# Two blocks of modulation rows of the even layer summed on VectorE instead of multiplied on TensorE

## Chip, cores and metric

One core of one Trainium2 chip. The metric is the device time of one execution in microseconds (us): three runs of a kernel and their median, and beside them one execution under the profiler, whose rows are quoted here.

## What is computed

The reference is a trunk of two layers over 512 tokens of width 1024. Each layer first turns the conditioning vector into six rows of modulation; rows 0 and 1 shift and scale the input of the mixer, row 2 gates its output, rows 3, 4 and 5 do the same for the experts.

```
c_act = jax.nn.silu(c)
for layer in range(DEPTH):
    mod = c_act @ ada_w[layer] + ada_b[layer]
    shift1, scale1, gate1, shift2, scale2, gate2 = jnp.split(mod, 6, axis=-1)
    h = modulate(rmsnorm(x, norm1_w[layer]), shift1, scale1)
    # layer 0: pooling mixer and chunked attention, layer 1: Mamba-2 mixer
    x = x + gate1[:, None, :] * mix
    h2 = modulate(rmsnorm(x, norm2_w[layer]), shift2, scale2)
    ffn = hier_moe(h2, ...)
    x = x + gate2[:, None, :] * ffn
```

`ada_w[layer]` is 1024 x 6144 in float32. The kernel cuts it into three parts of 2048 columns: part 0 holds shift1 and scale1, part 1 gate1 and shift2, part 2 scale2 and gate2.

## The kernel before

Everything is one program of five engines that run their own instruction streams in order and wait for each other by semaphores. The order within an engine is set once, when the program is built: a scheduler places the instructions by the order of the code and by its own costs. Only SP, ACT and POOL issue transfers.

**The even mixer** (`even_mixer`) works on four pairs of attention heads. For pair m it projects `q` and `k` (`Dense.next`, tiles `pdq`, `pdk`, 24 matmuls each, L449 to L452), forms the scores (`scores`, tile `sc`, L682), does the softmax (DVE L685 to L690, ACT L688), transposes the probabilities (`transp`, tile `ptr`, L700, copied out by ACT as `ptT`, L702), multiplies by the values (`values`, tile `po`, L711) and splits the result into a high and a low part (`c`, ACT L111 and DVE L112). Four pooling channels (tiles `pdu`, `pl`, `py`) lie between. Projection weights are split in the same way (`q3h`, `q3l` and the like; each third low part of this stage is done on POOL). At the end `out_proj` multiplies slices of the output weight (`mor`) by the gate row (L492), splits them (`mow0h`, `mow0l`) and multiplies on TensorE (tile `mo`).

**The modulation rows** come from the generator `ada(layer, part, eng)`, whose steps the calls of `fill()` drop between the steps of the mixer, by the table `FILL`. One block of 2048 columns is eight slices of 128 rows, 1 MB each, loaded two ahead into a ring of five buffers (tag `w8`). With `eng` None a step is one call of `ada_mm`: four matmuls, one for each 32 output partitions, that accumulate in the PSUM tile `pada`. With an engine given, the step is a running sum in place on that engine, and after one more step the partitions are summed by four matmuls with a matrix of ones:

```
if k:
    a = eng.scalar_tensor_tensor(ws[k], ws[k], ccol[:, k:k + 1], ws[k - 1], op0=ALU.mult, op1=ALU.add)
else:
    a = eng.tensor_scalar(ws[0], ws[0], ccol[:, 0:1], None, op0=ALU.mult)
```

Behind it, in both forms, DVE adds the bias (L215, tile `adab`). Part 0 then goes through four transposes (`pm`, L306) into the columns `ab` of `mod_cols`; parts 1 and 2 are written to the DRAM tile `modd`, and part 2 ends in `router_prep`, which reads `modd` back (`mc`), multiplies (`plb`, L249) and scales the router weights on DVE (L251). The bias tile `adab` and the gate row of `out_proj` share one buffer (tag `rows`). The expert weights `w_0_1` to `w_0_5` of the next stage use the same five `w8` buffers.

Part 1 of layer 0, part 2 of layer 0 and part 0 of layer 1 are computed in the even mixer, one after the other.

Of the kernel before, what the change touches and what calls it, by code (L numbers as in the profile page):

```python
# [76 lines left out]
def trunk_kernel(ctx, tc, x, c, ada_w, ada_b, norm1_w, norm2_w, mix_w_in, pool_w, pool_scale,  # L77
# [4 lines left out]
    V, S, GP, PE, SP = nc.vector, nc.scalar, nc.gpsimd, nc.tensor, nc.sync  # L82
# [7 lines left out]
    def w8(shape, name):  # L90
        return wp.tile(shape, F32, tag="w8", name=name, bufs=W8)
# [10 lines left out]
    def ps(shape=(P, 512), name="ps"):  # L102
        return pp.tile(list(shape), F32, tag="ps", name=name)

    def load_after(ins, first):

        if first is not None:
            tc.add_manual_dep(ins.ins, first.ins.name, SYNC, reason="load_after")
# [56 lines left out]
    def ada_mm(p, k, w, first, last):  # L165

        for q in range(4):
            PE.matmul(p[32 * q:32 * q + 32, :], ccol[:, k:k + 1].to_broadcast([P, 32]), w[:, q * 512:(q + 1) * 512],  # L168
                      start=first, stop=last, skip_group_check=True)

    def ada(layer, part, eng, first=None):


        rows = small.tile([P, D], F32, tag="rows", name=f"adab{layer}{part}", bufs=1)
        b = rows[:, 0:512]
        GP.memset(b, 0.0)
        SP.dma_start(b[0:P:32, :], ada_b[layer, part * 2048:(part + 1) * 2048].rearrange("(b n) -> b n", n=512))
        if part == 2:
            router_loads(layer)
            n2 = rows[:, 512:D]  # L180
            GP.memset(n2, 0.0)
            SP.dma_start(n2[0:64:32, :], norm2_w[layer].rearrange("(b n) -> b n", n=512))
        ws = {}

        def load(k):
            if k < KD:
                ws[k] = w8([P, 2048], f"ada{layer}{part}{k}")
                load_after(SP.dma_start(ws[k], ada_w[layer, k * P:(k + 1) * P, part * 2048:(part + 1) * 2048]), first)

        load(0)  # L190
        load(1)
        p = None
        for k in range(KD):
            load(k + 2)
            yield
            if not eng:
                if not k:
                    p = ps(name=f"pada{layer}{part}")
                ada_mm(p, k, ws.pop(k), k == 0, k == KD - 1)
                continue  # L200
# [4 lines that stand above are left out]
            if k in PIN:  # L205
                tc.keep_in_program_order(a)
        for _ in range(SLACK if eng else 0):
            yield
        if eng:
            p = ps(name=f"pada{layer}{part}")  # L210
            for q in range(4):
                PE.matmul(p[32 * q:32 * q + 32, :], ones[:, 0:32], ws[KD - 1][:, q * 512:(q + 1) * 512], start=True,
                          stop=True, skip_group_check=True)
        m = b
        V.tensor_add(m, p, b)  # L215
        if part == 0:
            mod_cols(layer, m)
        elif part == 1:
            SP.dma_start(modd[layer, 1], m[0:P:32, :])
        else:  # L220
            SP.dma_start(modd[layer, 2, 2:4], m[64:P:32, :])
            V.scalar_tensor_tensor(n2, m, 1.0, n2, op0=ALU.add, op1=ALU.mult)
            SP.dma_start(modd[layer, 2, 0:2], n2[0:64:32, :])
            yield from router_prep(layer)
# [5 lines left out]
    def router_loads(layer):  # L230
        d = rt[layer] = {"wr": small.tile([P, KD, NLOG], F32, tag="wr", name=f"wr{layer}", bufs=1)}
        d["mc"] = small.tile([P, 2, KD], F32, tag="mc", name=f"mc{layer}", bufs=1)
        d["lb"] = small.tile([P, NLOG], F32, tag="lb", name=f"lb{layer}", bufs=1)
        GP.memset(d["wr"], 0.0)
        GP.memset(d["lb"], -BIG)
        SP.dma_start(d["wr"][:, :, 0:4], moe_w_group[layer].rearrange("(p k) g -> p k g", k=KD))
        SP.dma_start(d["wr"][:, :, 8:NLOG], moe_w_expert[layer].rearrange("(p k) g e -> p k (g e)", k=KD))
        SP.dma_start(d["lb"][:, 0:4], dap(moe_b_group, 4 * layer, [[0, P], [1, 4]]))
        SP.dma_start(d["lb"][:, 8:NLOG], dap(moe_b_expert, 32 * layer, [[0, P], [1, 32]]))

    def router_prep(layer):
        d = rt[layer]
        for q, off in enumerate((4096, 3072)):
            SP.dma_start(d["mc"][:, q, :], dap(modd, layer * 6144 + off, [[KD, P], [1, KD]]))
        for _ in range(SLACK2):
            yield
        p = ps((P, NLOG), name=f"plb{layer}")
        for k in range(KD):
            PE.matmul(p, d["mc"][:, 1, k:k + 1].to_broadcast([P, P]), d["wr"][:, k, :], start=k == 0, stop=k == KD - 1)  # L249
        V.tensor_add(d["lb"], p, d["lb"])  # L250
        V.tensor_mul(d["wr"], d["wr"], d["mc"][:, 0, :, None].to_broadcast([P, KD, NLOG]))  # L251
# [51 lines left out]
    def mod_cols(layer, m):  # L303
        p = ps((P, 4, P), name=f"pm{layer}")
        for q in range(4):
            PE.transpose(p[:, q, :], m[:, q * P:(q + 1) * P], ident)  # L306
        A = ab[:, layer, 0, :].rearrange("p (b q) -> p b q", b=2)
        B = ab[:, layer, 1, :].rearrange("p (b q) -> p b q", b=2)
        V.scalar_tensor_tensor(A, p[:, :, 64::32].rearrange("p q b -> p b q"), 1.0,
                               n1w[layer].rearrange("p (b q) -> p b q", b=2), op0=ALU.add, op1=ALU.mult)  # L310
        V.tensor_copy(B, p[:, :, 0:64:32].rearrange("p q b -> p b q"))
# [201 lines left out]
    def even_mixer(layer):  # L513
        with ExitStack() as es:
# [217 lines left out]
            order = (0, 1, 4, 5, 6, 2, 7, 3)  # L732
            c_hi, c_lo = ({k: cs[n // 2][:, n % 2, q, :] for n, k in enumerate(order)} for q in range(2))

            adas = [ada(0, 1, None), ada(0, 2, None), ada(1, 0, None)]

            fills = iter(FILL)

# [716 lines left out]
    def odd_mixer(layer, prev):  # L1455
# [361 lines left out]
        return moe  # L1817

    moe = odd_mixer(1, even_mixer(0))
    fw = []  # L1820

# [55 lines left out]
```

## Time and profile before

| | us |
|---|---|
| three runs | 1078.89, 1082.63, 1082.91 |
| median | 1082.63 |
| the profiled execution, its own time | 1078.06 |
| its span, first to last instruction | 1076.4 |

The span is divided among stages: the even mixer ends and the output projection begins at about 203 us, the experts of layer 0 follow from about 272 us, the odd mixer from about 450 us. A row of a timeline gives the start, the duration, the engine, the line, what is written and read, how many instructions are merged, and in brackets how long the engine had been idle before and what ended that.

### The profile page before, as it was taken

To read this page: it belongs to the slowest core of one execution; us is meant where nothing else is said; L and a number is where in the kernel's file an instruction comes from. 1 tells how busy PE (TensorE), PEld (TensorE's weight loads), DVE (VectorE), ACT (ScalarE), POOL (GpSimd) and SP (SyncE) were. 2 spreads that over 40 slices of the span, in tenths; PEclk is the share of its full clock that TensorE was granted. 3 is DMA by queue.
4 is the path that set the end of the run, shared out by engine and by line. 5 is a ranking of instruction groups with operands and counts; after the bars stand their busy time and mean duration, and the time that the engine had idled before them with its cause. 6 is when DMAs were issued, how large, how long until landed. Compare 5 with 4: busy or idle time off the path is not lost. (4 is left out here: it accounts for less than half of the span.)

```text
span 1076.4 us, 15960 instructions
## 1 busy us (share of the span) xinstructions
PE 975.1 (91%) x5700; PEld 718.9 (67%) x5700; DVE 667.7 (62%) x1476; ACT 440.6 (41%) x893; POOL 219.9 (20%) x284
## 2 busy tenths in 40 slices
PE   5799998897899997899899999999969997998994
PEld 4576655686665656777787777878748876665653
DVE  3523443445556875758976699686766655654874
ACT  3434433324223235247475564664723234222332
POOL 3002110305231134200220131121130005221134
PEclk9899999998899999999999999999989998899997
DMA  8689856697799979547764387454236754799987
GB/s 313 240 280 313 287 219 268 243 369 255 234 386 414 409 210 298 187 122 229 236 182 129 107 235 245 127 150 144 79 118 222 267 194 159 261 411 414 411 258 182
DMA packets 137840, 263.88 MB, mean 245 GB/s; under 512 B 17555, under 2 KB 79975, under 8 KB 132632
## 3 DMA queue, kind: packets, MB, share of 16 engines
q1 hardware_dynamic: 126760, 235.36, 62.6%
q0 software_dynamic: 8928, 20.97, 7.4%
q10 hardware_dynamic: 2064, 6.42, 1.5%
q8 instruction: 49, 0.80, 0.3%
q14 instruction: 39, 0.32, 0.1%
HBM read 254.15 MB, written 20.11 MB: 255 GB/s over the span
## 5 line engine op out<-in xcount | busy, mean ns | idle before, releaser
L1063 PE MATMUL ph<-w,xT 128*64 128x256 f32 (+1 forms) x1152 | 132.0, 373 | 1.9 <-DVE xT L1047 1.6
L1063 PEld LDWEIGHTS ph<-w,xT 128*64 128x64 f32 x1152 | 86.4, 139 | 53.1 <-ACT xT L1049 9.5
L1065 ACT ACTIVATE th<-ph 128x128 f32<-128x128 f32 x34 | 9.4, 277 | 154.1 <-PE pht L1074 136.7
L1084 PE MATMUL pyy<-w,hidT 128*64 128x512 f32 x272 | 65.9, 605 | 2.2 <-ACT hidT L1076 2.2
L1030 POOL DMA_INDIRECT xg<-xnd,toks x32 | 32.2, 1007 | 150.8 <-PE pxt L1042 114.8
L1646 POOL TENSOR_TENSOR ms<-ms,cbm 128x512 f32<-128x512 f32 x16 | 27.1, 1709 | 167.9 <-DVE cbm L1618 116.9
L1049 ACT ACTIVATE xT<-pxt,mc 128x128 f32<-128x128 f32 x136 | 51.1, 456 | 17.4 <-PE pxt L1042 11.9
L1089 DVE SCALAR_TENSOR_TENSOR y<-pyy,wsl,gate 128x512 f32<-128x512 f32 x68 | 48.1, 745 | 9.2 <-DMA yd<-y 7.5
L1042 PE MATMUL pxt<-ident,xg 128*128 128x128 f32 x272 | 37.9, 284 | 15.0 <-DVEq L1415 8.6
L1047 DVE TENSOR_SCALAR xT<-pxt,mc 128x128 f32<-128x128 f32 x136 | 46.7, 405 | 1.4 <-PE pxt L1042 1.4
L1042 PEld LDWEIGHTS pxt<-ident,xg 128*128 128x128 f32 x272 | 34.5, 194 | 15.5 <-issue 15.1
L1115 DVE TENSOR_TENSOR x<-x,pyc 128x512 f32<-128x512 f32 x48 | 30.5, 684 | 22.6 <-DMA x<-yd,row 18.3
L1066 DVE SCALAR_TENSOR_TENSOR th<-th,ph 128x128 f32<-128x128 f32 x34 | 9.8, 287 | 55.2 <-ACT th L1065 55.2
L1631 ACT ACTIVATE ms<-lb,acs 128x128 f32<-128x128 f32 x128 | 40.0, 391 | 5.9 <-DMA lb<-acd 5.9
L1716 POOL TENSOR_TENSOR yy<-yy,yt 128x384 f32<-128x384 f32 x16 | 20.0, 1255 | 102.2 <-DVE yt L1714 81.2
L1595 DVE SCALAR_TENSOR_TENSOR cvx<-pdx,cw,cvx 128x511 f32<-128x511 f32 (+2 forms) x48 | 35.6, 742 | 2.4 <-ACT cvx L1592 2.2
L1210 POOL DMA_INDIRECT x<-yd,row x16 | 26.0, 1623 | 49.6 <-issue 24.0
L1084 PEld LDWEIGHTS pyy<-w,hidT 128*64 128x64 f32 x272 | 16.5, 136 | 26.0 <-issue 19.4
L202 DVE SCALAR_TENSOR_TENSOR ada<-ada,ccol,ada 128x2048 f32<-128x2048 f32 x14 | 33.6, 2403 | 0.1
L492 DVE TENSOR_TENSOR sor<-sor,gate 128x1024 f32<-128x1024 f32 x16 | 19.5, 1223 | 21.4 <-DMA sor<-in_ssm_w_out_dram 21.4
L1107 PE MATMUL pyc<-yh,yot 128*128 128x512 f32 x96 | 25.8, 397 | 2.9 <-DVE yot L1097 2.9
L168 PE MATMUL pada<-ada,ccol 128*32 128x512 f32 x192 | 24.9, 600 | 1.0 <-DMA ada<-in_ada_w_dram 1.0
(1087 smaller groups left out, 2667.4 us busy)
## 6 DMA issues: line engine op xcount, KB each, us to landing
w<-in_moe_w_dram SPq DMA_DIRECT2D x192, 512.0 KB
ada<-in_ada_w_dram SPq DMA_DIRECT2D x40, 1024.0 KB
yd<-y SPq DMA_DIRECT2D x22, 512.0 KB
ada<-in_ada_w_dram SPq DMA_DIRECT2D x16, 512.0 KB
wx<-in_ssm_w_in_dram SPq DMA_DIRECT2D x16, 512.0 KB
wz<-in_ssm_w_in_dram SPq DMA_DIRECT2D x16, 512.0 KB
lb<-acd SPq DMA_DIRECT2D x32, 256.0 KB
sor<-in_ssm_w_out_dram SPq DMA_DIRECT2D x16, 512.0 KB
```

The costliest lines, as they stand in the source:

```text
L202: a = eng.scalar_tensor_tensor(ws[k], ws[k], ccol[:, k:k + 1], ws[k - 1], op0=ALU.mult, op1=ALU.add)
L1030: d = GP.indirect_dma_start(out=xg, out_offset=None, in_=xnd[:, :], in_offset=bass.IndirectOffsetOnAxis(ap=idx, axis=0), bounds_check=T - ...
L1042: PE.transpose(p[:, q, :], xv[:, 4 * hf + q, :], ident)
L1047: V.tensor_scalar(xT[:, k, :], p[:, q, :], a, b, op0=ALU.mult, op1=ALU.add)
L1049: S.activation(xT[:, k, :], p[:, q, :], AF.Identity, bias=b, scale=a)
L1063: PE.matmul(ph[64 * j:64 * j + 64, n:n + h, :], xT[:, k, 64 * j:64 * j + 64], w13[n][:, :, k, :], start=k == 0, stop=k == KD - 1, skip_gro ...
L1084: PE.matmul(py[64 * j:64 * j + 64], hT[:, 64 * j:64 * j + 64], w2[:, s], start=True, stop=True, skip_group_check=True)
L1089: V.scalar_tensor_tensor(y[:, s], py, self.wsl[:, slot:slot + 1], self.gate2[:, s], op0=ALU.mult, op1=ALU.mult)
L1115: V.tensor_add(xst["x"][i][:, s], xst["x"][i][:, s], p)
L1595: V.scalar_tensor_tensor(a[:, sh:], p[:, :T - sh], cw[:, tap, ch:ch + 1], a[:, sh:], op0=ALU.mult, op1=ALU.add)
L1631: S.activation(ms[:, h, :], lb[:, h, :], AF.Relu, scale=-1.0, bias=acs[:, cq, 4 * g + h:4 * g + h + 1])
L1646: (V if cq % 2 else GP).tensor_mul(ms, ms, gs[g]["cbm"][:, cq, None, :].to_broadcast([P, 4, P]))
```

## The change

Of the three blocks in the even mixer the second and the third are given the engine V, DVE. Nothing else is edited.

```diff
-            adas = [ada(0, 1, None), ada(0, 2, None), ada(1, 0, None)]
+            adas = [ada(0, 1, None), ada(0, 2, V), ada(1, 0, V)]
```

In the built program 16 steps of four products leave TensorE, and 16 sums come to DVE (two of L204, fourteen of L202); two groups of four products with ones come to TensorE (L212). All orders differ from about the third pair's projections to the start of `out_proj`, and are the same before and after that.

TensorE behind the projection of `q` of the last pair, before: three steps of products (`ada_1110` and so on are weight slices), the router's `plb`, two steps of the next block, then the transposes of the third pair's probabilities.

```order
L452 MATMUL pdq_1295<-hhi_179,q3l 128x512
L168 MATMUL pada_1054<-ada_1110,ccol 32x512 x4
L168 MATMUL pada_1054<-ada_1138,ccol 32x512 x4
L168 MATMUL pada_1054<-ada_1210,ccol 32x512 x4
L249 MATMUL plb_1340<-wr_960,mc_961 128x40 x8
L168 MATMUL pada_1360<-ada_1354,ccol 32x512 x4
L168 MATMUL pada_1360<-ada_1356,ccol 32x512 x4
L700 MATMUL ptr_1373<-exch,pr_1215 128x128
```

The same place now:

```order
L452 MATMUL pdq_1279<-hhi_179,q3l 128x512
L212 MATMUL pada_1309<-ada_1194,ones 32x512 x4
L249 MATMUL plb_1320<-wr_960,mc_961 128x40 x8
L700 MATMUL ptr_1343<-exch,pr_1199 128x128
L700 MATMUL ptr_1347<-exch,pr_1199 128x128 x2
```

The five steps are gone; one group stands there that reads `ada_1194`, the slice in which the last sum of the block ends.

DVE behind the scaling of the router's weights, before (`sc` are the scores of the last pair of heads):

```order
L251 TENSOR_TENSOR wr_960<-wr_960,mc_961 128x320
L112 TENSOR_TENSOR c_549<-po_1470,c_549 128x512
L685 ISA scs_1493,mx_1492<-sc_1490,strip_1485 128x512
L685 ISA mx_1492 128x1
L687 TENSOR_SCALAR mx_1492<-mx_1492 128x1
L685 ISA scs_1502,mx_1501<-sc_1499,strip_1485 128x512
```

and now:

```order
L251 TENSOR_TENSOR wr_960<-wr_960,mc_961 128x320
L204 TENSOR_SCALAR ada_1334<-ada_1334,ccol 128x2048
L202 SCALAR_TENSOR_TENSOR ada_1336<-ada_1336,ccol,ada_1334 128x2048
L112 TENSOR_TENSOR c_549<-po_1430,c_549 128x512
L202 SCALAR_TENSOR_TENSOR ada_1338<-ada_1338,ccol,ada_1336 128x2048
L685 ISA scs_1450,mx_1449<-sc_1447,strip_1442 128x512
L685 ISA mx_1449 128x1
L202 SCALAR_TENSOR_TENSOR ada_1341<-ada_1341,ccol,ada_1338 128x2048
L687 TENSOR_SCALAR mx_1449<-mx_1449 128x1
L685 ISA scs_1459,mx_1458<-sc_1456,strip_1442 128x512
```

Two sums stand ahead of the split of the third pair's result, the other six between that split and the end of the softmax.

TensorE behind the last pooling projection `pdu` of `u3`, now; before, its transposes `ptr` of the last pair followed that projection at once, and the `pm` of this block stood ahead of the projections.

```order
L452 MATMUL pdu_1559<-hhi_179,u3l 128x512
L212 MATMUL pada_1599<-ada_1375,ones 32x512 x4
L306 MATMUL pm_1605<-ident,adab_1331 128x128 x4
L700 MATMUL ptr_1612<-exch,pr_1445 128x128
L700 MATMUL ptr_1616<-exch,pr_1445 128x128 x2
```

The end of the second running sum (`ada_1375`) and the columns made of it now stand ahead of the last transposes.

## Rows read from the trace of the kernel before

**Rows 1.** The page, part 1: the span.

```profile
span 1076.4 us, 15960 instructions
```

**Rows 2.** Busy time by stage: window, its length, busy us of each engine (instructions), PE clock, DMA.

```profile
116.00:142.00 26.00, 26.00 (x146) 15.60 (x142) 11.51 (x44) 12.36 (x31) 1.25 (x3) 1.00 0.81 278
142.00:181.00 39.00, 34.76 (x212) 19.25 (x210) 17.43 (x83) 15.05 (x43) 3.07 (x3) 0.99 0.63 251
```

**Rows 3.** The same windows, instructions on the tile pada alone: PE, PEld, DVE.

```profile
116.00:142.00 26.00, 6.15 (x40) 1.02 (x40) 0.00 (x0) 1.00 0.81 278
142.00:181.00 39.00, 11.09 (x88) 2.03 (x88) 1.38 (x2) 0.99 0.63 251
```

**Rows 4.** Tile ada, durations in ns (min/median/max), here from the odd layer.

```profile
L202 DVE SCALAR_TENSOR_TENSOR ada<-ada,ccol,ada x14: 2337/2344/3165, 493.1 to 666.6; 128x2048 f32<-128x2048 f32 x14
L204 DVE TENSOR_SCALAR ada<-ada,ccol x2: 1277/1280/1282, 491.2 to 616.3; 128x2048 f32<-128x2048 f32 x2
```

**Rows 5.** Timeline of DVE, 114 to 219 us.

```profile
114.86 0.69 DVE L685 CUSTOM_DVE_ANT_0 scs<-sc,strip 128x512 f32<-128x512 f32 x1
...
122.72 0.29 DVE L690 TENSOR_SCALAR pr<-scs,mx 128x128 f32<-128x128 f32 x1
123.04 0.69 DVE L112 TENSOR_TENSOR c<-plo,c 128x512 fp32r<-128x512 f32 x1
124.54 1.23 DVE L112 TENSOR_TENSOR k3l<-wk,k3h 128x1024 fp32r<-128x1024 f32 x1 [0.81 <-ACT k3h L111]
...
159.49 0.49 DVE L251 TENSOR_TENSOR wr<-wr,mc 128x320 f32<-128x320 f32 x1 [5.98 <-DMA mc<-modd]
170.81 0.69 DVE L112 TENSOR_TENSOR c<-po,c 128x512 fp32r<-128x512 f32 x1 [10.83 <-ACT c L111]
...
185.24 1.23 DVE L492 TENSOR_TENSOR mor<-mor,gate 128x1024 f32<-128x1024 f32 x1 [3.43 <-DMA gate<-modd]
...
218.41 2.58 DVE L492 TENSOR_TENSOR mor<-mor,gate 128x1024 f32<-128x1024 f32 x2 [7.48 <-DMA mor<-in_mix_w_out_dram]
```

**Rows 6.** Timeline of PE, 142 to 203 us.

```profile
142.30 0.50 PE L449 MATMUL pdq<-hhi,q3h 128*128 128x512 f32 x1
...
147.98 2.78 PE L168 MATMUL pada<-ada,ccol 128*32 128x512 f32 x24
150.69 1.98 PE L249 MATMUL plb<-wr,mc 128*128 128x40 f32 x16
...
164.60 1.25 PE L700 MATMUL ptr<-exch,pr 128*128 128x128 f32 x10
...
179.86 1.09 PE L306 MATMUL pm<-ident,adab 128*128 128x128 f32 x4 [3.12 <-DVE adab L215]
...
192.89 1.25 PE L700 MATMUL ptr<-exch,pr 128*128 128x128 f32 x10
...
198.13 2.37 PE L711 MATMUL po<-ptT,vsb 128*64 128x512 f32 x14 [1.02 <-ACT ptT L702]
202.24 1.10 PE L664 MATMUL py<-pl,pw 128*128 128x512 f32 x2 [1.74 <-DVE pl L659]
202.77 0.80 PE L457 MATMUL mo<-mow0h,c 128*128 128x512 f32 x1
```

**Rows 7.** Busy time by stage, behind the wait of 3.12 us: granted clock as a share.

```profile
180.00:182.00 2.00, 2.00 (x7) 1.74 (x8) 1.39 (x9) 0.50 (x2) 0.00 (x0) 0.50 0.05 12
182.00:184.00 2.00, 2.00 (x7) 1.58 (x6) 0.00 (x0) 0.00 (x0) 0.00 (x0) 0.67 0.92 223
```

**Rows 8.** Timeline of DVE, odd layer: a sum beside work on POOL.

```profile
618.60 3.17 DVE L202 SCALAR_TENSOR_TENSOR ada<-ada,ccol,ada 128x2048 f32<-128x2048 f32 x1
```

**Rows 9.** Timeline of POOL, odd layer: one addition alone, and two beside that sum.

```profile
509.00 1.01 POOL L1716 TENSOR_TENSOR yy<-yy,yt 128x384 f32<-128x384 f32 x1 [19.26 <-DVE yt L1714]
...
618.61 4.01 POOL L1716 TENSOR_TENSOR yy<-yy,yt 128x384 f32<-128x384 f32 x2 [6.90 <-DMA modd<-adab]
```

**Rows 10.** Timeline of SP, even layer: the load of the gate row.

```profile
180.98 0.33 SPq L463 DMA_DIRECT2D gate<-modd  x1
```

## The prediction

> **What bounds the kernel now.** The span is 1076.4 us [rows 1]; the only part of it in which anything changes lies between 116 and 203 us, the attention half of the even mixer. I read the stages first [rows 2]: TensorE is busy for 26.0 of 26 us and then for 34.8 of 39, DVE for 11.5 and 17.4. So TensorE bounds the stage and DVE is idle for 36.1 us of the 65. Of TensorE's time 6.15 + 11.09 = 17.2 us are the products of the two blocks that move [rows 3]; four products of a step run side by side, so it is the union that counts, not the sum of durations. So far the change looks good. But busy shares are averages, and both engines take their instructions in a fixed order, so I then walked along that order with the timelines of DVE [rows 5] and TensorE [rows 6]: what is to be seen there is where the two hand work to each other (scores to softmax, softmax to transposes, result to its split), and that the products before stood in the places where TensorE would have waited for DVE.
>
> **The change part by part.** *Removed:* 128 records of TensorE, 17.2 us [rows 3]. Sixteen come back as the two groups with ones, 17.2 / 8 = 2.2 us. Net 15.1 us of TensorE are freed; this is the most that the change can give.
>
> *Added:* two blocks of 1.28 + 7 x 2.34 = 17.7 us on DVE, from the same instructions in the odd layer [rows 4], 35.3 us in all. That is nearly all of DVE's idle time, so they can only be free if they fall into the right gaps. By the built order they don't.
>
> *The first block.* DVE has done the second pair's softmax and the pooling split at 123.04 + 0.69 = 123.7 [rows 5]. Then come five sums and two splits of weights (1.23 each [rows 5]): 1.28 + 4 x 2.34 + 2 x 1.23 = 13.1, to 136.8. The softmax of the third pair starts there. A softmax takes 114.86 to 123.0, 8.2 us [rows 5]; three sums and the split of the second pair's result (7.0 + 0.7) are laced into it, and the last sum ends when all but 0.7 of the softmax is done: 136.8 + 7.5 + 7.7 = 152.0. TensorE is early: it has no products to do, and the projection of the last q begins once DVE has read the first scores and made the split that frees a PSUM bank (two times 0.69 after 136.8, 138.2), and takes 5.7 (142.30 to 147.98 [rows 6]), to 143.9. Its next instruction is the group that reads the last sum. It **waits for DVE for some 9 us**, in a place where before it had five steps of products and no wait.
>
> *A sum beside POOL.* A sum that ran beside POOL's additions took 3.17 instead of 2.34 [rows 8], and two additions on POOL 4.01, where one alone takes 1.01 [rows 9]. In the new stage POOL has one split of weights beside the first block and three additions beside the second. The price of a sum that meets POOL is 0.8; the unknown is how many do: none at the least, four at the most (3.3 us). I take one in each block, as POOL has work for only 3.07 us of 39 there [rows 2]. The first block so ends at 152.8. [...]
>
> *The clock.* [...] I charge 1.7 behind the first wait, and in the second double the 1.06 of the ones group. [...]
>
> *The third pair to its split.* From 152.8: ones 1.06, `plb` 1.98, transposes 1.25, projection 5.7, half clock 1.7: 11.7. From the second transposes to the end of the split it was 164.60 to 171.5, less one step of products, 5.8 [rows 5, 6]. So DVE has split the third result at 170.3; before it was 171.5. A gain of 1.2 is all that is left of the thirteen steps that have gone by then. The wait of DVE for `mc` (5.98 [rows 5]) now holds sums up, but is hidden: two sums behind it end at about 165, and DVE then waits for that split anyway.
>
> *The second block and the last softmax.* Six sums (14.0), the last softmax (8.2), the pooling combination (0.7), less 0.4 behind the last sum, and 0.8 for POOL: 23.3 us, to 193.6. TensorE starts its last two projections when the first scores are read (170.3 + 2.34 + 0.69) and ends them at 173.3 + 11.4 = 184.7. **A second wait of 9 us.** Then ones at half clock 2.1, bias 0.7, `pm` 1.1: the last transposes start at 197.5. Before they started at 192.89. From there to `mo` it took 9.9; the wait of 1.74 for pooling goes (its projections are done 8 us earlier), and `py` fits into the wait for `ptT` (0.5): 7.6, so `mo` starts at 205.1. Before: 202.77 [rows 6].
>
> *The gate row* shares its buffer with the bias tile. It was issued at 180.98 [rows 10], when `pm` was done, and DVE used it 4.3 us later [rows 5]. Now `pm` ends at 197.5, so the gate is used at 201.8; multiplication 1.2 and high part 1.1 end at 204.1, one microsecond before it matters.
>
> **Sum.** `mo` starts 2.3 us later, and all that follows has the same order and moves with it: 1078.06 + 2.3 = 1080.4 for the profiled execution. That one is 4.6 below the median of the three runs and 0.8 below the fastest; the mean of the four is 1080.6, and 2.3 above it is 1082.9. I forecast **1083 us, no change that can be measured**: 0.5% is 5.4 us here, about what a measurement of this kernel can tell. With the bounds (no clock cost and no meeting with POOL: 4.4 less; four meetings: 1.7 more; full clock cost twice: 0.6 more) this case alone spans 1078 to 1087.
>
> **Rivals.** *The sums slip under TensorE's work* (0.13). If DVE reached the ends of both blocks before TensorE asks, TensorE would keep its 15.1 us: 1083 - 2 - 15 = 1066, and with half of it 1073. For it speaks that DVE's idle time (36.1) is as long as the sums (35.3). Against it, that one sum chain is serial, starts only when the second softmax is over, and that each wait I find is 9 us, more than the sums could be wrong by: they would have to take 1.2 us less each in the first block.
>
> *The output projection starves* (0.22, slower). The loads of `w_0_1` to `w_0_5` wait for the buffers of the sums, are all issued at the end of the second block, and stand on SP ahead of the gate row and of all but the first two slices of `mor`. A slice that stood behind expert weights kept DVE idle for 7.48 [rows 5] where the gate kept it for 3.43. If the gate is 4 us later than I take it, `mo` starts 3.0 later (1.0 is spare); the third slice of `mor` gets its buffer only when the first is split, and as late as that it costs another 1 to 3. It decides as soon as the gate row takes more than 5.3 us from its issue. Then 2.3 + 3 + 1 to 3, with the most meetings with POOL 8 to 10: 1088 to 1091.
>
> *The forecast* keeps 0.65.
>
> **Numbers.** Slower by over 0.5% is above 1088.0: 0.2 from the starving case and 0.02 from the top of mine, 0.22. Faster is below 1077.2: the first rival, 0.13. The range leaves out half of the first rival and the tails of the other: 1072 to 1093. The forecast's own range is 1078 to 1087.
>
> **What would show it.** In the new profile: `pada` on TensorE idle for 7 to 10 us before each of two groups on line 212 and released by DVE line 202; a clock of 0.5 behind both; the split of the third pair's result within 2 us of 170; the last `ptr` at 195 to 199; `mo` at 203 to 207; SP's gate load at about 197. Without waits above 3 us there, or with `mo` before 198, I am wrong; with DVE idle above 5 us before the first `mor`, the starving case holds.

## The result, and the profile after

The changed kernel takes **1088.2 us** (median of 8 runs, 1083.9 to 1092.2); the kernel before, run beside it, 1079.1. The ratio is 1.0075 [1.0054, 1.0097]: slower by 8 us. The forecast was 1083, +2.3 us and "no change that can be measured". The time lies in the range of 1072 to 1093 and just above the forecast's own (1078 to 1087); the direction is the one to which the text gave 0.22.

Page of the kernel after, span and first lines of part 1 (busy us, share of the span, instructions); before, the span was 1076.4 [rows 1], PE was busy for 975.1 us and DVE for 667.7:

```profile
span 1087.3 us, 15759 instructions
PE 972.8 (89%) x5588; PEld 727.9 (67%) x5588; DVE 702.3 (65%) x1492; ACT 441.6 (41%) x893; POOL 219.7 (20%) x284
```

DVE has 34.6 us more, as foreseen (35.3). TensorE, which was to lose 15.1, has 2.3 less: part of its work now runs at half clock (0.50 in the windows further down; mean granted clock of the profile 0.951, before 0.969). Timeline of TensorE after, where [rows 6] stood before (start, duration, engine, line, operation, tiles, size, records, idle time before it and what ended that):

```profile
138.62 0.50 PE L449 MATMUL pdq<-hhi,q3h 128*128 128x512 f32 x1
...
152.79 1.93 PE L212 MATMUL pada<-ada,ones 128*32 128x512 f32 x8 [8.43 <-DVE ada L202]
154.65 3.64 PE L249 MATMUL plb<-wr,mc 128*128 128x40 f32 x16
...
194.28 1.94 PE L212 MATMUL pada<-ada,ones 128*32 128x512 f32 x8 [8.17 <-DVE pl L659]
197.02 1.11 PE L306 MATMUL pm<-ident,adab 128*128 128x128 f32 x4 [0.81 <-DVE adab L215]
197.93 2.34 PE L700 MATMUL ptr<-exch,pr 128*128 128x128 f32 x10
200.06 1.91 PE L664 MATMUL py<-pl,pw 128*128 128x512 f32 x2
...
205.12 2.37 PE L711 MATMUL po<-ptT,vsb 128*64 128x512 f32 x14
207.41 1.65 PE L457 MATMUL mo<-mow0h,c 128*128 128x512 f32 x6
```

The two waits are there, 8.43 and 8.17 us (forecast: 9 and 9). The second is put down to `pl`; but the group reads the last sum, which ends at 191.79 + 2.35 = 194.14. Timeline of DVE after:

```profile
135.01 2.35 DVE L202 SCALAR_TENSOR_TENSOR ada<-ada,ccol,ada 128x2048 f32<-128x2048 f32 x1
...
147.95 2.25 DVE L690 TENSOR_SCALAR pr<-scs,mx 128x256 f32<-128x256 f32 x2
150.40 2.34 DVE L202 SCALAR_TENSOR_TENSOR ada<-ada,ccol,ada 128x2048 f32<-128x2048 f32 x1
...
171.30 0.69 DVE L112 TENSOR_TENSOR c<-po,c 128x512 fp32r<-128x512 f32 x1 [5.29 <-ACT c L111]
...
180.10 2.35 DVE L202 SCALAR_TENSOR_TENSOR ada<-ada,ccol,ada 128x2048 f32<-128x2048 f32 x1
182.36 1.29 DVE L690 TENSOR_SCALAR pr<-scs,mx 128x512 f32<-128x512 f32 x1
...
191.79 2.35 DVE L202 SCALAR_TENSOR_TENSOR ada<-ada,ccol,ada 128x2048 f32<-128x2048 f32 x1
```

And the clock behind the waits, in windows of TensorE's execution (core busy times, then PEclk as the third number from the end, the share of full speed):

```profile
154.00:156.00 2.00, 2.00 (x11) 1.35 (x7) 1.17 (x2) 0.00 (x0) 0.20 (x1) 0.50 0.68 279
158.00:160.00 2.00, 2.00 (x11) 2.00 (x11) 0.20 (x1) 1.01 (x3) 0.53 (x1) 0.50 0.83 295
...
198.00:200.00 2.00, 2.00 (x11) 2.00 (x10) 0.24 (x2) 1.15 (x3) 1.72 (x2) 0.50 0.83 309
200.00:202.00 2.00, 2.00 (x6) 0.86 (x5) 0.00 (x0) 0.60 (x1) 0.00 (x0) 0.51 0.81 279
202.00:204.00 2.00, 2.00 (x12) 1.08 (x11) 1.62 (x4) 1.99 (x6) 0.00 (x0) 1.00 0.61 236
```

The two executions are not at the same point at 60 us, so I count lateness from the first `pdq` of the program, which no version changes (62.47 before, 63.28 after). By that count `mo` is 3.8 us late, not 2.3, and the end of the span is **10.1 us late**: more than half of the loss in this profile arises after the stage in which anything was changed. The experiments had two questions: do the sums make the loss at `mo`, and what makes the rest.

### The profile page after: what moved, and what is told of

Its sections match the earlier page's. It is cut to its first block, busy times and chain, and to the rows that moved or that the text cites. A ratio compares the mean times of both kernels' runs of the same rounds, so it can differ in the third digit from the quotient of the medians.

```text
span 1087.3 us, 15759 instructions
## 1 busy us (share of the span) xinstructions
PE 972.8 (89%) x5588; PEld 727.9 (67%) x5588; DVE 702.3 (65%) x1492; ACT 441.6 (41%) x893; POOL 219.7 (20%) x284
## 5 line engine op out<-in xcount | busy, mean ns | idle before, releaser
L1063 PEld LDWEIGHTS ph<-w,xT 128*64 128x64 f32 x1152 | 88.6, 141 | 52.6 <-issue 10.2
L202 DVE SCALAR_TENSOR_TENSOR ada<-ada,ccol,ada 128x2048 f32<-128x2048 f32 x28 | 65.7, 2345 | 0.2
L688 ACT ACTIVATE scs<-scs,mx 128x512 f32<-128x512 f32 (+3 forms) x32 | 17.9, 559 | 33.7 <-DVE mx L687 33.4
(1087 smaller groups left out, 2680.8 us busy)
```

Source lines behind the costliest of these rows:

```text
L1063: PE.matmul(ph[64 * j:64 * j + 64, n:n + h, :], xT[:, k, 64 * j:64 * j + 64], w13[n][:, :, k, :], start=k == 0, stop=k == KD - 1, skip_gro ...
```

## The experiments

All results first. Lateness is in us against the profile of the kernel before, counted as above, at the start of `mo`, at the first `pgn` of the odd mixer (588 us before) and at the end of the span; one profile each. The ratio comes from several timed runs beside the kernel before.

| version | mo | pgn | end | ratio to before, interval |
|---|---|---|---|---|
| changed kernel | 3.8 | 7.8 | 10.1 | 1.0075 [1.0054, 1.0097] |
| the same again | 3.5 | 9.5 | 11.2 | one time, 1088.4 beside 1076.7 |
| second block only | 0.9 | -3.1 | -2.1 | 1.0001 [0.9982, 1.0020] |
| third block only | 3.1 | 2.6 | 4.9 | 1.0038 [1.0021, 1.0055] |
| first block only | -1.9 | -3.8 | -2.7 | 0.9983 [0.9968, 0.9997] |
| sums of half length | -13.4 | -13.7 | -17.3 | one time, 1060.4 beside 1077.1 |
| clock kept up | 2.4 | 0.6 | 1.6 | 1.0067 [1.0042, 1.0092] |
| first block, first five on DVE | 5.7 | 5.8 | 6.2 | 1.0071 [1.0050, 1.0092] |
| three blocks in part | 12.7 | 9.8 | 11.4 | 1.0129 [1.0108, 1.0151] |
| first block, last five on DVE | -7.2 | -7.8 | -6.2 | 0.9967 [0.9948, 0.9986] |
| first and second in part | -7.1 | -6.9 | -2.9 | 0.9963 [0.9942, 0.9985] |
| before, mo delayed (4) | 0.8 | 0.6 | 0.0 | 0.9999 [0.9979, 1.0020] |
| before, mo delayed (6) | 2.6 | 2.9 | 2.3 | 1.0040 [1.0017, 1.0062] |

**One block at a time.**

```diff
-            adas = [ada(0, 1, None), ada(0, 2, V), ada(1, 0, V)]
+            adas = [ada(0, 1, None), ada(0, 2, V), ada(1, 0, None)]
```

> Only part 2 of layer 0 (the second of the three blocks) is summed on DVE; part 0 of layer 1 is multiplied on TensorE as before. Theory W (each block costs the wait of TensorE for the end of its serial chain of sums): the first wait stays as in the changed kernel, 8 us before the group with ones at about 153, plb ends at about 158 where it ended at 152.7 before, and the products of the next block stand behind it again. mo then starts 3 to 5.6 us later than in the kernel before, total 1.003 to 1.005 of it. Rival F (what counts is the work taken off TensorE, and the loss comes from something after the mixer): 8.5 us of products go, 1.1 come, mo starts some 7 us earlier, total 0.994 or better.

Measured, TensorE's timeline:

```profile
152.68 1.94 PE L212 MATMUL pada<-ada,ones 128*32 128x512 f32 x8 [8.41 <-DVE ada L202]
...
187.60 0.66 PE L306 MATMUL pm<-ident,adab 128*128 128x128 f32 x4 [0.87 <-DVE adab L215]
```

The wait of 8.4 us and `plb` are as in the changed kernel, `mo` is 0.9 late, the time 1.0001 of before. Neither number of theory W (3 to 5.6) nor of F (-7) came. The first wait is fully there: the second transposes of the third pair (164.60 in [rows 6]) are 6.0 late. But products now stand behind it, and the built order has moved `pm` from ahead of both pooling projections to between them: its wait is 0.87 instead of the 3.12 of [rows 6], with no half clock behind (`pm` took 0.66 instead of 1.09).

```diff
+            adas = [ada(0, 1, None), ada(0, 2, None), ada(1, 0, V)]
```

> Only part 0 of layer 1 (the third block) is summed on DVE. Theory W: nothing changes up to 150; the third pair's result is split some 6 us earlier than before (about 164), then six sums (14 us) are laced into the last softmax (8.2), the last sum ends at about 188, TensorE is done with the pooling projections at about 178 and waits some 9 us; the last transposes start at 191 to 193, mo at 201 to 203 (before: 202.8), total 0.998 to 1.001. Rival F: mo some 7 us earlier, 196, total 0.994 or better.

Measured: TensorE's timeline with the third block alone on DVE:

```profile
184.12 1.94 PE L212 MATMUL pada<-ada,ones 128*32 128x512 f32 x8 [11.08 <-DVE ada L202]
187.74 1.09 PE L306 MATMUL pm<-ident,adab 128*128 128x128 f32 x4 [1.69 <-ACT scs L688]
196.17 1.25 PE L700 MATMUL ptr<-exch,pr 128*128 128x128 f32 x10
```

A wait of 11.1 where 9 were expected, and behind it a whole projection (between `pm` and `ptr`), most of it at half clock (0.50 from 180 to 192). `mo` is 3.1 late: W in kind, 3 to 5 us too low in size. The second and third block together (0.9 + 3.1) come near the 3.8 of the changed kernel at `mo`; as `pm` stands between the projections in these two and behind both in the changed kernel, that may be chance.

```diff
+            adas = [ada(0, 1, V), ada(0, 2, None), ada(1, 0, None)]
```

> Only part 1 of layer 0 (the first of the three blocks) is summed on DVE; its sums stand between the first softmax and the second, where DVE has nothing else but two splits and the pooling tail, and none is laced into a softmax. Theory W: the sums run from about 91 to 114, TensorE waits some 4 us for the group with ones, the second softmax starts no later than before, and the products of the other two blocks stand where TensorE waits for the later softmaxes: mo 2 to 4 us earlier than before, total 0.996 to 0.998. Rival F: 7.4 us earlier, 0.993. Rival D (any block on DVE costs more than it frees, wherever it stands): mo later than before, total above 1.002.

Measured: `mo` 1.9 early, 0.9983 [0.9968, 0.9997]. That is near theory W's 0.996 to 0.998, and rival D's (above 1.002) did not come. TensorE's timeline:

```profile
115.89 0.79 PE L682 MATMUL sc<-kT,qT 64*128 64x128 f32 x2 [6.47 <-DVE c L112]
...
165.58 1.25 PE L700 MATMUL ptr<-exch,pr 128*128 128x128 f32 x10
...
185.18 0.66 PE L306 MATMUL pm<-ident,adab 128*128 128x128 f32 x4 [0.87 <-DVE adab L215]
```

But the sums did cost something. TensorE waits for 6.47 us before its last scores, since the split of the first pair's result, which frees a bank, stands behind the sums; and at the second transposes of the third pair (165.58, before 164.60) this version is still 1.4 us late by the common count. The gain comes behind that place: here too `pm` has moved between the projections, waits 0.87 instead of 3.12 and takes 0.66 instead of 1.09. No version moves `pm` alone, so what that is worth by itself was not tested.

**How much of it are the sums?**

```diff
-        p = None
+        p, W = None, slice(0, 1024 if layer == 0 or part == 0 else 2048)
...
-                a = eng.scalar_tensor_tensor(ws[k], ws[k], ccol[:, k:k + 1], ws[k - 1], op0=ALU.mult, op1=ALU.add)
+                a = eng.scalar_tensor_tensor(ws[k][:, W], ws[k][:, W], ccol[:, k:k + 1], ws[k - 1][:, W], op0=ALU.mult, op1=ALU.add)
...
-                a = eng.tensor_scalar(ws[0], ws[0], ccol[:, 0:1], None, op0=ALU.mult)
+                a = eng.tensor_scalar(ws[0][:, W], ws[0][:, W], ccol[:, 0:1], None, op0=ALU.mult)
```

> Both blocks on DVE as in the changed kernel, but each of their 16 sums runs over 1024 of the 2048 columns; what the other half of gate2 of layer 0 and scale1 of layer 1 would be is left out. The loads stay whole. A sum then takes about 1.2 us instead of 2.34. Theory W (the sums as work of DVE set the ends of both blocks): the two waits of TensorE before the groups with ones shrink from 8.4 and 8.2 to under 3 each, the last transposes start at 183 to 188 instead of 197.9, mo at 194 to 198 instead of 207.4. Rival L (the loads of the slices set the ends, 1 MB at some 370 GB/s is 2.8 us, longer than a sum): the waits stay above 6 us and now DVE waits for DMA before the sums. Rival F: waits shrink, but the time of the experts' first units after mo stays behind as in the changed kernel (4.5 us later at mo, 7.8 at the fourth unit), by 3 us more than mo itself.

Measured: TensorE's timeline with sums of half length, and DVE's:

```profile
143.27 1.06 PE L212 MATMUL pada<-ada,ones 128*32 128x512 f32 x8
...
176.07 1.50 PE L212 MATMUL pada<-ada,ones 128*32 128x512 f32 x8 [4.45 <-DVE ada L202]
...
188.97 1.90 PE L457 MATMUL mo<-mow0h,c 128*128 128x512 f32 x7
```

```profile
127.80 3.92 DVE L202 SCALAR_TENSOR_TENSOR ada<-ada,ccol,ada 128x1024 f32<-128x1024 f32 x3
133.76 1.28 DVE L202 SCALAR_TENSOR_TENSOR ada<-ada,ccol,ada 128x1024 f32<-128x1024 f32 x1 [0.91 <-DMA ada<-in_ada_w_dram]
...
169.50 2.08 DVE L202 SCALAR_TENSOR_TENSOR ada<-ada,ccol,ada 128x1024 f32<-128x1024 f32 x1
```

The first wait is gone, the second 4.45, and `mo` starts 13.4 us earlier than before: 17 us earlier than with whole sums, for 15 us less work on DVE (busy for 687.3 instead of 702.3). That is further than theory W's 194 to 198, and the second wait is above its 3. One wait for a load, 0.91: rival L falls. So at `mo` the cost comes from DVE's work: in these two places DVE, not TensorE, sets the end. It is not simply one for one, since with the first wait the half clock behind it is gone too (ones and `plb` at 1.06 and 1.98). (The time of the whole run isn't compared, as later stages see other values.)

**Is the clock behind the waits a large part?** Seven products that nothing uses stand ahead of each group with ones:

```diff
-            p = ps(name=f"pada{layer}{part}")
+            p = ps(name=f"pada{layer}{part}"); [PE.matmul(p, ones, q, start=True, stop=True, skip_group_check=True) for q in warm]
...
+            warm.extend(7 * [vsb[:, 0, :]]); adas = [ada(0, 1, None), ada(0, 2, V), ada(1, 0, V)]
```

> The changed kernel with seven products of 128x512 that nothing uses (about 1.05 us each) ahead of each of the two groups with ones, in the places where TensorE waited 8.4 and 8.2 us; the order of all else on TensorE is the same. Theory C (the half clock behind the waits is a large part of the loss): ones, plb and the transposes behind the first wait take 1.06, 1.98 and 1.25 instead of 1.93, 3.64 and 2.37, the third pair's result is split 3.6 us earlier, and behind the second wait another 3.3 us come back (ones, pm, transposes, py): mo at 200 to 202 instead of 207.4, total 0.999 to 1.003 of the kernel before. Rival W (the waits alone set the time, what follows them waits for DVE anyway): mo not before 205, total 1.005 to 1.009.

Measured, TensorE's timeline:

```profile
143.34 6.17 PE L210 MATMUL pada<-vsb,ones 128*128 128x512 f32 x14
151.95 1.06 PE L212 MATMUL pada<-ada,ones 128*32 128x512 f32 x8 [2.44 <-DVE ada L202]
152.94 3.41 PE L249 MATMUL plb<-wr,mc 128*128 128x40 f32 x16
...
194.90 1.06 PE L212 MATMUL pada<-ada,ones 128*32 128x512 f32 x8 [2.68 <-DVE ada L202]
196.78 0.66 PE L306 MATMUL pm<-ident,adab 128*128 128x128 f32 x4 [0.81 <-DVE adab L215]
197.27 1.26 PE L700 MATMUL ptr<-exch,pr 128*128 128x128 f32 x10
```

The seven took 6.17, less than the 7.3 I had taken, and the wait of 2.44 that was left halved the clock again at `plb` (3.41 instead of 1.98): the first half of the test failed. Behind the second wait the clock stayed up, and ones, `pm`, `ptr` and `py` gave back 0.88 + 0.45 + 1.08 + 0.89 = 3.3, as expected. But `mo` gained 1.4 only, since DVE ended its sums 1.5 us later by the common count. So rival W's numbers came (`mo` not before 205, 1.005 to 1.009), though for a reason of its own: the first half clock was still there. The ratio, 1.0067, can't be told from 1.0075.

**A piece where DVE is idle.** A block may be split: some slices summed, the rest multiplied into the same PSUM tile, the ones added to it (`sums` and `on` are the slices on DVE).

```diff
+            if k >= n:
...
+                ada_mm(p, k, ws.pop(k), k == n, k == KD - 1)
+                if n and k == n + 1:
+                    for q in range(4):
+                        PE.matmul(p[32 * q:32 * q + 32, :], ones[:, 0:32], ws[n - 1][:, q * 512:(q + 1) * 512],
+                                  start=False, stop=False, skip_group_check=True)
...
+            adas = [ada(0, 1, V, sums=5), ada(0, 2, None), ada(1, 0, None)]
```

> Of part 1 of layer 0 (the first block) five of the eight slices are summed on DVE and three multiplied on TensorE into the same PSUM tile, with the group of ones between them; the other two blocks as before. With all eight slices TensorE waited 6.5 us because the first pair's split stood behind the sums. Theory W (a sum costs nothing where it ends before TensorE comes to what stands behind it): the five sums end at about 105, no wait above 1.5 us, 5 x 1.06 - 1.06 = 4.2 us come off TensorE, mo 3 to 4.5 us earlier than before, total 0.996 to 0.997. Rival G (what frees the start of mo is something else, the gate row or the pooling chain on POOL): mo 2 us earlier at the most, total 0.998.

Measured, TensorE's timeline:

```profile
98.44 1.94 PE L168 MATMUL pada<-ada,ccol 128*32 128x512 f32 x8 [6.28 <-DMA ada<-in_ada_w_dram]
```

Both theories missed: 5.7 late, 1.0071. The sixth slice takes the buffer of the first, and that is free only when the second sum has read it (93.5; the load was issued then); so the slow consumer held up the load that the fast one waits for. The same in all three blocks was worse, with two such waits (6.2 and 5.4), and 4.9 before `pm`:

```diff
+            adas = [ada(0, 1, V, sums=5), ada(0, 2, V, sums=3), ada(1, 0, V, sums=3)]
```

> All three blocks in part: the first five slices of the first block, the first three of the second and of the third are summed on DVE, the rest multiplied on TensorE. The sums are meant for the three stretches in which DVE idles between softmaxes (91 to 113, 125.8 to 134.3, 154 to 170). Theory W: TensorE loses 4.2 + 2.1 + 2.1 = 8.4 us of products and waits nowhere over 2 us, mo 6 to 8.5 us earlier than before, total 0.992 to 0.995. Rival G (gate row, output weights or pooling hold mo back): mo 2 to 4 us earlier, total 0.997. Rival D (a sum delays the softmax behind it): a wait of TensorE over 4 us before transposes of the third or the last pair, total above 0.998.

Measured: `mo` 12.7 late, 1.0129. None of the three theories has it: the long waits are for loads and before `pm`, not before the transposes of a softmax.

Turned round, with the products first and the sums last:

```diff
+            adas = [ada(0, 1, V, on=(3, KD)), ada(0, 2, None), ada(1, 0, None)]
```

> Of the first block TensorE multiplies the first three slices, DVE sums the last five, and the group with ones closes the PSUM tile after the scores of the second pair. In the run with the first five on DVE TensorE waited 6.3 us for the load of the sixth slice, whose buffer the second sum had freed only at 95; here the three products free their buffers at 87. Theory R (that wait came from the ring of five buffers): no wait for a load, at most 1 us before py, the 4.2 us of five products less the ones come off, mo 3 to 4.2 us earlier than before, total 0.996 to 0.997. Rival G (the gate row or the pooling chain holds mo, whatever is freed): mo 2 us earlier at the most, total 0.998 or above.

Measured, TensorE's timeline:

```profile
111.53 1.07 PE L173 MATMUL pada<-ada,ones 128*32 128x512 f32 x8
...
178.75 0.66 PE L311 MATMUL pm<-ident,adab 128*128 128x128 f32 x4 [0.87 <-DVE adab L220]
184.72 1.25 PE L705 MATMUL ptr<-exch,pr 128*128 128x128 f32 x10
...
193.68 0.80 PE L462 MATMUL mo<-mow0h,c 128*128 128x512 f32 x1
```

TensorE has no wait for a load and none for the ones; theory R holds. At the second transposes of the third pair this version is 3.7 early, the 3 to 4.2 that R expected. At `mo` it is 7.2 early: here too the order has put `pm` between the projections, and its wait (3.12 before) and the half clock behind it go as well (`pm` took 0.66 instead of 1.09). The first number is what the five sums gave. The time is 0.9967 [0.9948, 0.9986], or 3.6 us: half of what is gained at `mo`.

```diff
+            adas = [ada(0, 1, V, on=(3, KD)), ada(0, 2, V, on=(0, 3)), ada(1, 0, None)]
```

> As the run before, and of the second block the first three slices are summed on DVE, in its idle stretch from 126 to 134 between the second softmax and the third; the other five are multiplied, and the third block is as in the kernel before. In the run with all three blocks in part this second piece alone gave 1.9 us between the scores of the second pair and the router's products. Theory R: another 1.9 to 2.1 us, mo 5 to 6.3 us earlier than before, total 0.994 to 0.996. Rival D (a sum delays the softmax beside it by as much as TensorE gains): no more than the run before, total 0.996 or above.

Measured: `mo` 7.1 early, as much as with the first piece alone, 0.9963 [0.9942, 0.9985]. Rival D: the three sums delay the second softmax, whose transposes now wait twice (0.31 and 0.61), and the second piece adds nothing. These two versions beat the kernel before by 0.3 to 0.4%; which of the two is better can't be told.

**Where does the rest come from?**

> The changed kernel once more, unedited. Its first profile had mo at 207.41 and the fourth unit of the experts at 316.67, 109.3 apart, where the kernel before has 106.1, the second block alone 104.5 and the third alone 106.1. Theory P (the extra 3.2 us belong to that one execution: a clock that rose late in the first unit and one late instruction of ACT): 104 to 107 apart this time. Theory S (they follow from the change, because 2.4 MB fewer of the expert weights have been loaded by 240 us): 109 apart again, with TensorE at half clock in the first unit's second group of 32 products and a wait of about 1 us in the fourth unit.

Measured: 313.82 - 205.29 = 108.5, between the two theories; at the end of the span it is again 11.2 late. One ACT instruction, `th` in the experts of layer 0, is again 1.4 us late, and 1.0 of it stays; it is so too in the five versions from "clock kept up" to "first and second in part" and in none of the others, and the rows don't settle what it waits for. Of the profiles whose chip is on record, these six were all taken on one chip and the others on two more, so this piece may go with the chip and not with the change. The larger piece lies in the odd mixer, where lateness rises by 3.9 and 5.7 between 494 and 588. (Between 400 and 494 it had fallen by 3.1 and 2.1, and it falls there in every version: the one profile of the kernel before loses time in that stretch.) The first part of the rise is a wait before `pdx`, 1.11 before, 1.84 in the changed kernel and 2.74 in its repeat, in both with half clock behind (0.59 and 0.56 from 502 to 506, and 0.52 and 0.62 from 500 to 504); no other version rises by over 1.6 there. Timelines of the kernel before and of the changed one:

```profile
496.13 0.50 PE L449 MATMUL pdx<-sh_hi,x10h 128*128 128x512 f32 x1 [1.11 <-DVE cvb L1595]
```
```profile
501.58 0.50 PE L449 MATMUL pdx<-sh_hi,x10h 128*128 128x512 f32 x1 [1.84 <-DVE cvb L1595]
```

The second part follows `pxd`, before which every version waits in much the same way. Timelines of the kernel before and of the changed one, each followed by its windows:

```profile
526.07 0.88 PE L1659 MATMUL pxd<-ident,cvx 128*128 128x128 f32 x6 [3.24 <-ACT cvx L1598]
```
```profile
526.00:528.00 2.00, 1.93 (x12) 1.71 (x13) 1.96 (x2) 1.94 (x4) 0.00 (x0) 1.00 1.11 275
528.00:530.00 2.00, 2.00 (x11) 1.64 (x10) 2.00 (x6) 0.00 (x0) 0.00 (x0) 1.00 0.94 352
```
```profile
533.10 1.54 PE L1659 MATMUL pxd<-ident,cvx 128*128 128x128 f32 x6 [3.18 <-ACT cvx L1598]
```
```profile
532.00:534.00 2.00, 0.90 (x4) 0.90 (x5) 1.96 (x2) 1.99 (x5) 0.00 (x0) 0.77 1.02 295
534.00:536.00 2.00, 2.00 (x8) 1.71 (x7) 2.00 (x3) 0.97 (x2) 0.00 (x0) 0.50 1.03 295
```

The same wait of 3.2 us left the clock at 1.00 before and took it to 0.50 after. To see whether that belongs to the sums, the kernel before got a delay of `mo` and nothing else (the second run has 6 in the place of the 4):

```diff
-                py = ps(name=f"py{g}")
+                py = ps(name=f"py{g}"); [PE.matmul(py, pw[:, g, :], vsb[:, 0, :], start=True, stop=True) for _ in range(4 if g == 3 else 0)]
```

> The kernel before (no block on DVE), with four products of 128x512 that nothing uses (about 0.9 us each) on TensorE around the last transposes of the even mixer, ahead of the last pooling product; apart from neighbours that change places among DVE's and SP's work for the output weights the order is the same. mo starts 1 to 3 us later. In the changed kernel mo was 3.5 to 4.6 us later and the end 10 us; on the way the wait of 3.2 us before pxd, which is there in the kernel before too, put the clock from 1.00 to 0.50 for some 4 us. Theory H (what the later waits cost depends on the moment at which they fall, any shift of the start can bring it about): the lateness against the kernel before does not stay at that of mo, it changes by over 1.5 us on the way, up or down, where the clock differs behind the same waits. Theory B (the late stages lose because of the sums themselves, by the expert weights that were loaded later): the lateness of mo is kept within 0.7 us to the end, and the clock behind pxd stays at 1.00.

> As the run before with six such products: mo 3 to 5 us later than in the kernel before. Theory H: the lateness again does not stay at that of mo, and changes by another amount than with four products; total between 0.999 and 1.009. Theory B: it stays within 0.7 us, total 1.003 to 1.005.

Measured, the same place in the two runs:

```profile
524.62 1.54 PE L1659 MATMUL pxd<-ident,cvx 128*128 128x128 f32 x6 [3.96 <-ACT cvx L1598]
```
```profile
526.15 1.54 PE L1659 MATMUL pxd<-ident,cvx 128*128 128x128 f32 x6 [3.20 <-ACT cvx L1598]
```

With four, lateness is 0.8 at `mo` (1 to 3 expected), -2.1 at 494, 0.6 at 588; with six 2.6 (3 to 5), -1.5, 2.9. Both fall to half clock behind `pxd` (0.59 and 0.56 from 524 to 528 with four, 0.50 from 526 to 532 with six), without a sum in the even mixer, so theory B falls for this place. It does not set the changed kernel apart either: at or just behind `pxd` the granted clock falls to 0.50 in twelve of the fourteen profiles, also in those that end early, and stays at 1.00 only in the kernel before and with the clock kept up. Theory H is not shown by it. Each lateness compares two single executions, and the 19 timed runs of the kernel before beside these two, with no shift at all, lie between 1071.9 and 1082.2.

Both delayed versions end within 0.8 of where they were at `mo`, and the changed kernel doesn't: twice it ended 6 to 8 us later than at `mo`, where no other profile gained over 4.2. The timed runs add something that the profiles hide. The profile with the clock kept up gained nothing, but it is the fastest of that version's six runs (1079.56, median 1081.94). By its ratio that version loses 7.2 us, 4.8 more than it is late at `mo`; the changed kernel loses 8.1, 4.3 more. The intervals reach from 2 to 7.5. For the two delayed versions the same difference is -0.9 and 1.7, and can't be told from nothing. So the two versions with both blocks whole on DVE lose alike behind `mo`, and theory B, the loads of the expert weights, is not excluded for that loss.

The mean granted clock of each timed run says what kind of loss it is. It is 0.948 to 0.954 in the eight runs of the changed kernel (mean 0.951), 0.957 to 0.964 with the clock kept up (0.960), and 0.962 to 0.969 (0.9665) in the eleven runs of the kernel before beside that version and the repeat. As an estimate, with every lost share taken as time at 0.50: 107, 87 and 72 us at half clock. Between 60 us and `mo` the three traces have 27, 10 and 3 us. Behind it that leaves 11 and 8 us more than in the kernel before, which cost half of that at the most, 5.6 and 3.8 us: about the 4.3 and 4.8 to be explained. So the loss behind `mo` looks like half clock in later stages, in the runs at large and not in two unlucky ones. What brings it about stays open.

## Why the prediction was right or wrong

*The waits: right.* First sums end 152.7 (forecast 152.8), second 194.1 (193.6); waits 8.4 and 8.2 (9 and 9). The changed profile is 0.8 late before all this; less that, the third pair's split begins at 170.5, where I had it done at 170.3, and the last transposes start at 197.1 (197.5).

*The clock: mis-sized.* I had charged 1.7 behind the first wait and 1.1, at the ones alone, behind the second. Measured: 0.87 + 1.66 + 1.12 = 3.7 for ones, `plb` and transposes, and 0.88 + 1.09 + 0.89 = 2.9 for ones, `ptr` and `py`, with 0.50 up to 161 and 202 us. No run shows 1.7 as the price of such a wait: it was my estimate, half of the 3.4 us at half clock (179.9 to 183.3) behind the one wait of 3.12 us [rows 6, 7], and the bound "full clock cost twice" rested on it too; behind waits of 8 the low clock lasted some 8 us each time. How long it lasts I took from that one place, and that was the error.

*"From there to mo 7.6":* it took 9.5, and the second half of the clock's price is just that difference (1.09 + 0.89 = 2.0). The pooling terms were right: the waits for `pl` and `ptT` are gone.

*Meetings with POOL.* Priced at 0.8 each, two taken, 1.6 in all. In the changed kernel no sum grew: all took 2.34 or 2.35. The sum at 180.10 kept its time, and the addition on POOL that began beside it took 1.71, where one alone takes 1.06 in this trace:

```profile
181.65 1.71 POOL L654 TENSOR_TENSOR pss<-pu 128x527 f32<-128x527 f32 x1 [23.05 <-ACT pu L649]
```

The `pr` that began beside that addition took 1.29 instead of 0.49, and the two at 147.95, begun beside a split on POOL, 2.25, where two such take 0.54: 2.5 us in all. Sums can pay too: with half sums one that began beside POOL took 2.08 instead of 1.28. In these meetings it was the instruction that began second that lasted longer, and the prediction had charged the sums whatever the order. It had also charged sums alone, which read two tensors; here `pr`, with one tensor input, took 0.80 longer. Which instructions of DVE lose time beside POOL the rows don't settle.

*"All that follows has the same order and moves with it": the step that failed.* It carries the larger part of the miss: 3.8 late at `mo`, 10.1 at the end of the profile, 8.1 by the timed runs. The order is the same but in the first slice of the output weight, where high products have gone ahead of low ones; the next slice begins 3.6 late, so that is not the step. What the later waits cost is not the same: before `pdx` TensorE waited for 1.84 and 2.74 instead of 1.11, and the time at half clock behind `mo` is longer in the timed runs, by about what is lost. Why it is longer stays open.

*The rivals.* The output projection did not starve: `gate` was issued at 198.2 and the first `mor` multiplied at 204.0, in time for `mo`. So "slower" came true by another road than the one that held its chance, and that the time lies in the range of 1072 to 1093 is luck: the upper part of that range was laid for the case that did not come. How the sums slip under TensorE's work the run with half sums shows: at half length the first wait goes, and the second is still 4.45.

## What to carry to other kernels

Moving work to an engine that is idle on average pays only for the part that fits into its idle stretches between things that others wait for: a block of the same size made TensorE wait for 6.5, 8.4 or 11.1 us in three places, and five of the eight slices of one, put where nothing waited, gave 3.7 us. A change of this kind also moves other instructions: where the order put `pm` between the projections, its wait fell from 3.12 to 0.87, and a gain at `mo` must not be put down to the sums without looking at that. If two engines share the slices of one ring, as here, the fast one had better take its slices first, or it waits for buffers that the slow one holds (6.28 us with the sums first, nothing with the products first). And a forecast of some us in a kernel with waits needs a range for the stages behind the change too: the versions lost up to 5 us there by the timed runs.

## What was not expected of the hardware

The same wait of TensorE, 3.2 us before the same instruction, was followed by a granted clock of 1.00 in the kernel before and with the clock kept up, and of 0.50 in the changed kernel, in both delayed ones (4.0 and 3.2 us) and, behind 3.2 to 3.5 us, in all the other versions. What decides it is not in these rows. Even 1.84 us before `pdx` was followed by half clock in the changed kernel (0.59 and 0.56 from 502 to 506, products of 0.63 us), and 2.74 at the same place in the kernel with `mo` delayed (6) was not (products of 0.39 and 0.40). And beside POOL a DVE instruction that began second was stretched, a TENSOR_SCALAR from 0.49 to 1.29 us, while the sum that had begun first kept its 2.35.
